# Attention's products with the values: one group for a head's 512 queries in place of two groups of 256

## The chip, the cores and the metric

The kernel runs on one core of a Trainium2 chip. The metric is the device time of one execution in microseconds; three runs of the kernel before gave 909.68, 910.4 and 912.59, median 910.4. The profile is one further execution, taken by the hardware profiler. In it PE is TensorE's matmul, PEld its weight load, DVE VectorE, ACT ScalarE, POOL GpSimd and SP SyncE, which only issues DMAs here.

## The reference

One encoder block on 512 tokens of width 2048. A modulated RMS norm is projected into two mixers that run side by side: dilated window attention with 16 heads of 64, and a gated linear attention with 4 heads. Both are gated, concatenated, projected, added to the input through a gate and normalised. The change is in the attention:

```python
for window, dilation in DILATED_PATTERNS:          # (128,1), (512,4), (2048,16)
    o_p, lse_p = dilated_window_attention(aq, ak, av, rel_bias, window, dilation)
mix_w = jax.nn.softmax(jnp.stack(lses, axis=0), axis=0)
att = jnp.einsum('pbsh,pbshe->bshe', mix_w.astype(av.dtype), jnp.stack(outs, axis=0))
```

Three softmaxes that are merged by their denominators are one softmax over a row's keys, in which a key counts as often as patterns contain it. So for each head the kernel needs scores, one softmax, and the product of its weights with the values, out[query] = sum over keys of p[query, key] v[key].

## The kernel before

**Precision.** A product of two float32 matrices is made from parts: a high part that ACT writes as fp32r, and a low part that DVE gets by subtracting it. The projections take three products (high by high, high by low, low by high). For the values, vv holds in its 128 stationary columns both parts side by side (64 high, 64 low), and the probabilities are multiplied part by part. The two halves of the output's partitions are added at the end.

**Stages.** The start (condition sums, norm, the projection of the values and of four heads' queries and keys) takes until about 187 us. Then four units follow, qk2, qk4, qk6 and gk. Each is a projection of 192 products of 512 columns, and each carries the attention of four heads. Later units (values and gates of the linear attention, then the output projection) take the rest.

**Tokens and tiles.** Tokens are sorted by parity (the queries' order is the reverse of the keys'); a tile i is 128 queries. Of 512 keys a tile needs 416: three whole chunks of 128 and a rest of 32. Tile 0 has chunks 1, 2, 3 and a rest in chunk 0; tile 1 chunks 2, 3, 0 and a rest in 1; tile 2 chunks 3, 0, 1 and a rest in 2; tile 3 chunks 0, 1, 2 and a rest in 3.

**A head's work.** Each of these is an item of the list that attention() makes:
- score (lines 819 to 856): two products of 416 columns into a PSUM tile s; two DVE operations add the bias and take the minimum (L837), ACT takes the exponential (L841), DVE the reciprocal (L844), POOL the scaling (L854). With a score goes one piece of side work for DVE, a token sum (S) or a sum for the value bias (vbias).
- turn (858 to 876): three transposes on PE into t (L871); ACT writes the high part (L875), DVE the low part (L876). The turn of tile 3 first does rest (879 to 890): one transpose r of the four 32-key rests (L882), two copies on ACT (L888), two subtractions on DVE (L890), and the same again.
- values (892 to 907): for each pair of tiles e, eight products of 256 columns (L899), four chunks by two parts, from a tile pts[e] that holds both parts and has blocks of zeros where a tile has no keys in the chunk. The rests come last. Then ACT copies half of the output (L902) and DVE adds it to the other half into cat (L906).

**What sets the order.** PE's instructions stand as the program is written. A unit counts a tick for every three of its 192 products, and an item is put in when its place, spread evenly from 0.185 on over 0.8 of the unit, is reached; the last one falls into the next unit. On the other engines a scheduler of the framework orders the instructions when the program is built, and each runs its queue in order. SP issues its DMAs in order too. PSUM has three buffers for s, t and o together. Weights are fetched by SP, split by ACT (L491) and DVE (L475), some groups of 24 products ahead.

Of the kernel before, what the change touches and what calls it, by code (L numbers as in the profile page):

```python
# [18 lines left out]
P = 128  # L19
S = 512  # L20
D = 2048
KT = D // P
# [57 lines left out]
def _runs():  # L80
# [109 lines left out]
def block_kernel(ctx: ExitStack, tc: tile.TileContext, a: dict):  # L190
    nc = tc.nc
# [7 lines left out]
    sm = mid.enter_context(tc.tile_pool(name="sm", bufs=4))  # L199
# [303 lines left out]
    spl, psb, vraw, vv, sqs = {}, {}, {}, {}, {}  # L503
# [131 lines left out]
    for i, (st, k) in enumerate(sets[1:], 1):  # L635
        e = "ab".index(st)
# [15 lines left out]
    for z in range(2):  # L652
        c = slice(512 * z, 512 * z + 512)
# [31 lines left out]
    n = len(chain) // 2  # L685
# [54 lines left out]
    ident = const("ident", [P, P])  # L740
# [49 lines left out]
    cat = [None] * 4  # L790
# [13 lines left out]
            return go[1]()  # L804

    pts = []

    def attention(pairs):

        tiles = [(2 * p + j, i) for p in pairs for j in range(2) for i in range(4)]  # L810
        gt, pr_ = {}, {}
        heads = [2 * p + j for p in pairs for j in range(2)]

        def g_load(h):
            g = gp.tile([P, 896], F32, tag="g", name=f"g{h}")
            nc.sync.dma_start(g[:, :768], bass.AP(grow.tensor, grow.offset + h * 1024, [[2, P], [1, 768]]))
            gt[h] = g

        def score(h, i):
            def go():  # L820
# [12 lines left out]
                st = sm.tile([P, 4], F32, tag="st", name=f"st{h}{i}", bufs=6)  # L833
                least = 3e38
                for z, (lo, hi, at) in enumerate(BIAS_AT[i]):
                    to = st[:, 0:1] if hi == NK else st[:, 3:4]
                    top = nc.vector.tensor_tensor_reduce(  # L837
                        out=t[:, lo:hi], in0=ps[:, lo:hi], in1=gt[h][:, at:at + 2 * (hi - lo) - 1:2], op0=ALU.add, op1=ALU.min,
                        scale=1.0, scalar=least, accum_out=to).ins
                    least = to  # L840
                act(t, t, AF.Exp, bias=st[:, 0:1], scale=-1.0, accum_out=st[:, 1:2])  # L841
                held = beside(top)
                with tc.issue_after(held) if held else nullcontext():
                    nc.vector.reciprocal(st[:, 2:3], st[:, 1:2])  # L844
                todo_ = [(t, t)]
                if i % 2:
                    todo_ = [(t[:, :384], t[:, :384]), (pr_[h, 0][:, 96 - 32 * i:128 - 32 * i], t[:, 384:416])]
                elif i:
                    todo_ = [(t[:, 32:], t[:, 32:]), (pr_[h, 0][:, 32:64], t[:, :32])]
                for to, of in todo_:  # L850
                    if (h, i) in ((15, 2), (15, 3)):
                        act(to, of, AF.Copy, scale=st[:, 2:3])
                    else:
                        last["pool"] = nc.gpsimd.tensor_scalar(to, of, st[:, 2:3], 1.0, op0=ALU.mult, op1=ALU.mult).ins  # L854
                pr_[h, i] = tile_
            return go

        def turn(h, i):
            def go():
                e, half = divmod(i, 2)  # L860
                if len(pts) == e:
                    pts.append(B8(f"pt{e}", [2, 4, 256], F32R))
                    nc.gpsimd.memset(pts[e][:, :, 3, 0:P].bitcast(F32), 0.0)
                    nc.gpsimd.memset(pts[e][:, :, 0, P:2 * P].bitcast(F32), 0.0)
                if i == 3:
                    rest(h)
                pt, t = pts[e], pr_.pop((h, i)) if i else pr_[h, i]
                pk = PA(f"t{h}{i}")
                first_ = 0 if half else 128
                for kt in range(3):  # L870
                    nc.tensor.transpose(pk[:, kt * P:kt * P + P], t[:, first_ + kt * P:first_ + kt * P + P], ident)  # L871
# [3 lines left out]
                act(hi, src, AF.Copy)  # L875
                tt(lo, src, hi.bitcast(F32), op=ALU.subtract)  # L876
            return go

        def rest(h):

            pk = PJ(f"r{h}")
            nc.tensor.transpose(pk[:, :P], pr_.pop((h, 0))[:, 0:128], ident)  # L882
            for e in range(2):
                at = 64 - 64 * e
                of = pk[at:at + 32, :P], pk[at + 32:at + 64, :P]
                to = [(pts[e][0:32, w, 0, P:2 * P], pts[e][96:128, w, 3, 0:P]) for w in range(2)]
                for z in range(2):
                    act(to[0][z], of[z], AF.Copy)  # L888
                for z in range(2):
                    tt(to[1][z], of[z], to[0][z].bitcast(F32), op=ALU.subtract)  # L890

        def values(h, e):
            def go():
                t = pts[e]
                po = PA(f"o{h}{e}")
                order = (1, 2, 3, 0)
                for n_, c in enumerate(order):
                    for w in range(2):
                        mm(po[:, :256], vv[h // 4][:, CHUNK_OF[e][c], h % 4, :], t[:, w, c, :],  # L899
                           start=n_ == 0 and w == 0, stop=n_ == 3 and w == 1)  # L900
                oh = sm.tile([64, 256], F32, tag="oh", name=f"oh{h}{e}", bufs=1)
                act(oh, po[64:128, :256], AF.Copy)  # L902
                own = stacks[h][3]
                p = h // 2
                dst = cat[p // 4][own, p % 4, :].rearrange("p (c e) -> p e c", e=2)[:, 1 - e, :]
                tt(dst[:, ::-1], po[0:64, :256], oh, op=ALU.add)  # L906
# [48 lines left out]
    def shift_row():  # L955

        pt_ = PA("pshift")
        nc.tensor.transpose(pt_[:KT, :P], shift, ident)
        t = sm.tile([KT, P], F32, tag="oh", name="shiftt", bufs=1)
# [708 lines left out]
    for pair, (l, r) in enumerate(OUT_PAIRS):  # L1668
# [17 lines left out]
        v = keep(f"v{pair}", g1)  # L1686
# [100 lines left out]
```

## Time and profile before

| | |
|---|---|
| runs | 909.68, 910.4, 912.59 us; median 910.4 |
| the profiled execution, first to last instruction | 907.1 us (its own time around this is not told) |
| granted PE clock | 0.997 |
| PE busy | 893.3 us, 98% |
| DVE busy | 730.9 us, 81% |
| ACT busy | 498.2 us, 55% |
| the four units with attention | 187 to 445 us |

Busy PE time is not PE at its peak: products overlap, and a row's duration is longer than the distance to the next. How long an instruction occupies PE is read from start to start. In rows of the timeline the columns are start, duration, engine, line, operation, output and inputs, shapes, count, and in brackets the idle time ahead of it with what ended it.

### The profile page before, as it was taken

The page shows a single profiled execution, that of the slowest core. Times are in us where ns is not written, and L with a number is a line of the kernel's source. Part 1 is how long each engine was busy: PE and PEld are TensorE (multiplying, and loading weights), DVE is VectorE, ACT ScalarE, POOL GpSimd, SP SyncE. Part 2 cuts the span into 40 slices and gives each one's busy share as a digit, 9 for nine tenths or more (in the row PEclk, how much of TensorE's full clock was granted, in tenths as well). Part 3 has the DMA queues.
Part 4 walks back from the last instruction along what each step waited for, and adds up shares of the span by engine and source line. Part 5 has one row for each costly group of instructions (what it writes and reads, how often), then busy time and mean ns, then how long its engine had stood idle before and what let it go on. Part 6 is the DMA issues. An engine that isn't in the chain of part 4 may idle for free.

```text
span 907.1 us, 12545 instructions
## 1 busy us (share of the span) xinstructions
PE 893.3 (98%) x4279; PEld 744.4 (82%) x4279; DVE 730.9 (81%) x1236; ACT 498.2 (55%) x859; POOL 120.8 (13%) x218
## 2 busy tenths in 40 slices
PE   8999999999999999999999999999999999999996
PEld 6888888888888888888878888888888888888884
DVE  7998899878889888888668668595787559797787
ACT  5553533566656755656657554373664248455464
POOL 0000000023323233133100101112020100000001
PEclk9999999999999999999999999999999999999998
DMA  9999498587797897998878869678797987877863
GB/s 350 403 413 405 177 370 308 172 249 215 218 267 244 233 261 226 251 271 229 281 232 258 316 201 314 204 241 267 234 277 206 277 282 284 291 284 255 298 231 145
DMA packets 64203, 241.30 MB, mean 266 GB/s; under 512 B 8358, under 2 KB 10694, under 8 KB 54538
## 3 DMA queue, kind: packets, MB, share of 16 engines
q1 hardware_dynamic: 57378, 198.18, 61.2%
q0 software_dynamic: 6464, 42.01, 19.6%
q8 instruction: 34, 0.56, 0.2%
q10 hardware_dynamic: 296, 0.30, 0.1%
q14 instruction: 31, 0.25, 0.1%
HBM read 224.64 MB, written 51.47 MB: 304 GB/s over the span
## 4 chain that ended last, share of the span: by engine, by line
PE 55%; DVE 2%; ACT 1%; issue 1%; DVEq 0%; ACTq 0%
PE g L230 4%; PE g L228 4%; PE g L229 4%; PE ps_ag L230 3%; PE ps_ag L228 3%; PE ps_ag L229 3%; PE ps_gv_P L228 3%; PE ps_gv_P L229 3%; PE ps_gv_P L230 3%; PE ps_gg L228 2%; PE ps_gg L229 2%; PE ps_gg L230 2%; PE go L1102 2%; PE ps_gk L228 2%; PE ps_gk L229 2%; PE ps_gk L230 2%
## 5 line engine op out<-in xcount | busy, mean ns | idle before, releaser
L854 POOL TENSOR_SCALAR p<-p,st 128x32 f32<-128x32 f32 (+2 forms) x108 | 55.0, 519 | 167.4 <-DVE st L844 120.7
L326 DVE CUSTOM_DVE_ANT_0 cb<-cb,sb,c_bcond 128x2048 f32<-128x2048 f32 (+1 forms) x32 | 73.4, 2295 | 1.9 <-DMA cb<-in_wm 1.7
L841 ACT ACTIVATE p<-p,st 128x416 f32<-128x416 f32 x64 | 41.1, 642 | 46.7 <-DVE st L837 38.9
L427 POOL DMA_DIRECT2D T<-in_w_o x32 | 23.1, 724 | 159.2 <-ACT V2h L491 10.8
L876 DVE TENSOR_TENSOR pt<-t,pt 128x384 fp32r<-128x384 f32 x64 | 35.3, 551 | 3.9 <-ACT pt L875 3.0
L875 ACT ACTIVATE pt<-t 128x384 fp32r<-128x384 f32 x64 | 31.3, 488 | 12.7 <-PE t L871 11.7
L899 PEld LDWEIGHTS o<-pt,vv 128*128 128x128 f32 x256 | 34.9, 190 | 3.7 <-DVE pt L890 0.6
L899 PE MATMUL o<-pt,vv 128*128 128x256 f32 x256 | 36.3, 283 | 0.3 <-DVE pt L890 0.2
L871 PE MATMUL t<-c_ident,p 128*128 128x128 f32 x192 | 31.3, 272 | 0.0
L871 PEld LDWEIGHTS t<-c_ident,p 128*128 128x128 f32 x192 | 24.3, 140 | 7.9
L837 DVE CUSTOM_DVE_ANT_0 p<-s,g,st 128x256 f32<-128x256 f32 x64 | 27.6, 432 | 1.7
L837 DVE CUSTOM_DVE_ANT_0 p<-s,g 128x160 f32<-128x160 f32 x64 | 23.4, 366 | 4.9 <-PE s L830 3.9
L829 PE MATMUL s<-ks,qh 128*128 128x416 f32 x64 | 22.9, 358 | 0.3 <-DVE pt L876 0.3
L326 DVE CUSTOM_DVE_ANT_0 rawg<-rawg,crow,gate 128x1024 f32<-128x1024 f32 x16 | 20.4, 1280 | 2.9 <-DMA rawg<-in_wg 2.9
L830 PE MATMUL s<-ks,ql 128*128 128x416 f32 x64 | 22.4, 351 | 0.0
L1070 ACT ACTIVATE sq<-st,sc 128x256 f32<-128x256 f32 x24 | 12.2, 506 | 18.4 <-DVE st L1060 9.9
L427 POOL DMA_DIRECT2D T3V<-in_w_gv x8 | 5.5, 684 | 126.0 <-ACT qk21h L491 119.8
L1560 POOL TENSOR_SCALAR x<-x,rn 128x512 f32<-128x512 f32 x2 | 2.3, 1168 | 148.2 <-ACT rn L1549 143.7
L888 ACT ACTIVATE pt<-r 32x128 fp32r<-32x128 f32 x64 | 17.1, 268 | 8.2 <-DVE pt L890 3.4
L326 DVE CUSTOM_DVE_ANT_0 rawg<-rawg,crow,c_bcond 128x1024 f32<-128x1024 f32 x16 | 20.3, 1278 | 0.7 <-DMA rawg<-in_wg 0.7
L890 DVE TENSOR_TENSOR pt<-r,pt 32x128 fp32r<-32x128 f32 x64 | 18.2, 285 | 1.8 <-ACT pt L888 0.7
L427 POOL DMA_DIRECT2D T<-T x16 | 8.9, 559 | 79.3 <-ACT V8h L491 12.9
(1660 smaller groups left out, 3115.3 us busy)
## 6 DMA issues: line engine op xcount, KB each, us to landing
cb<-in_wm SPq DMA_DIRECT2D x31, 1024.0 KB, 8.7
T<-in_w_o POOLq DMA_DIRECT2D x32, 512.0 KB, 6.3
rawg<-in_wg SPq DMA_DIRECT2D x32, 512.0 KB, 6.0
raw_O<-in_w_o SPq DMA_DIRECT2D x32, 512.0 KB, 4.7
raw_qk<-in_w_qk SPq DMA_DIRECT2D x24, 512.0 KB, 4.3
raw_O<-T SPq DMA_DIRECT2D x24, 512.0 KB, 5.5
rawb<-in_w_sb SPq DMA_DIRECT2D x16, 512.0 KB, 5.5
rawv<-in_wv SPq DMA_DIRECT2D x16, 512.0 KB, 4.8
```

What stands on the lines that cost most here:

```text
L228: mm(ps, lh, rh, start=first, stop=False, skip_group_check=more)
L229: mm(ps, ll, rh, start=False, stop=False, skip_group_check=more)
L230: mm(ps, lh, rl, start=False, stop=last, skip_group_check=more)
L326: return nc.vector.tensor_tensor_reduce(out=w, in0=w, in1=with_, op0=ALU.mult, op1=ALU.add, scale=1.0, scalar=init, accum_out=dst)
L427: move = nc.gpsimd.dma_start(dst, src, max_dma_last_dim=8192, **how).ins
L837: top = nc.vector.tensor_tensor_reduce(out=t[:, lo:hi], in0=ps[:, lo:hi], in1=gt[h][:, at:at + 2 * (hi - lo) - 1:2], op0=ALU.add, op1=ALU.min,
L841: act(t, t, AF.Exp, bias=st[:, 0:1], scale=-1.0, accum_out=st[:, 1:2])
L854: last["pool"] = nc.gpsimd.tensor_scalar(to, of, st[:, 2:3], 1.0, op0=ALU.mult, op1=ALU.mult).ins
L871: nc.tensor.transpose(pk[:, kt * P:kt * P + P], t[:, first_ + kt * P:first_ + kt * P + P], ident)
L875: act(hi, src, AF.Copy)
L876: tt(lo, src, hi.bitcast(F32), op=ALU.subtract)
L899: mm(po[:, :256], vv[h // 4][:, CHUNK_OF[e][c], h % 4, :], t[:, w, c, :], start=n_ == 0 and w == 0, stop=n_ == 3 and w == 1)
```

## The change

A head's probabilities now lie in two tiles, one for the high part and one for the low part, with 16 slots of 128 queries each, so that the tiles' blocks for one key chunk stand at equal distances. One group of nine products makes all 512 queries of a head: chunks 1 and 2 for all four tiles (512 columns, both parts), chunk 0 for tiles 1 to 3 and chunk 3 for tiles 0 to 2 (384 columns, both parts). The rests of tiles 1 and 2 stand in slots 11 and 2 among whole blocks, with 96 rows of zeros. The rests of tiles 0 and 3 get slots 14 and 15: there both parts stand below each other in one tile's rows, and a ninth product of 256 columns multiplies them with rest_v, which holds those 32 rows of the values twice. Four DMAs of 32 rows a unit fill rest_v from vv. Output copy and addition are done once a head, for 512 columns; the copy's buffer now comes from the pool of general 512-column tiles. An item list of 36 replaces that of 40.

```diff
-CHUNK_OF = ((1, 2, 3, 0), (3, 0, 1, 2))
+FULL = (((2, 0), (3, 5), (1, 10)), ((2, 1), (0, 4), (3, 7)), ((0, 6), (3, 9), (1, 12)), ((2, 3), (0, 8), (1, 13)))
+RUN_OF = ((1, 0, 4, 10, 1), (2, 0, 4, 0, 1), (0, 1, 4, 4, 2), (3, 0, 3, 5, 2))
+REST_OF = (14, 11, 2, 15)
...
+    def rest_load(w):
+        t = rest_v[w] = kp.tile([P, 4, P], F32R, tag="rv", name=f"rv{w}")
+        for z in range(4):
+            of = vv[w][96:128, 0] if z < 2 else vv[w][0:32, 3]
+            nc.sync.dma_start(t[32 * z:32 * z + 32].bitcast(F32), of.bitcast(F32))
...
-                e, half = divmod(i, 2)
-                if len(pts) == e:
-                    pts.append(B8(f"pt{e}", [2, 4, 256], F32R))
...
+                if not pts:
+                    for z in "hl":
+                        pts.append(B8(f"pt{z}", [16, P], F32R))
...
-                hi = pt[:, 0, half:half + 3, P * half:P * half + P]
-                lo = pt[:, 1, half:half + 3, P * half:P * half + P]
+                at, step = FULL[i][0][1], FULL[i][1][1] - FULL[i][0][1]
+                hi, lo = (pt[:, at:at + 2 * step + 1:step, :] for pt in pts)
...
+            hi, lo = pts
+            to = [(hi, 0, hi, 32), (hi, 0, lo, 0), (hi, 96, lo, 96), (hi, 64, hi, 96)]
+            parts = [(t[a:a + 32, REST_OF[i], :], u[b:b + 32, REST_OF[i], :], pk[96 - 32 * i:128 - 32 * i, :P])
+                     for i, (t, a, u, b) in enumerate(to)]
+            for pair in (parts[:2], parts[2:]):
+                for up, _, of in pair:
+                    act(up, of, AF.Copy)
+                for up, low_, of in pair:
+                    tt(low_, of, up.bitcast(F32), op=ALU.subtract)
...
-        def values(h, e):
+        def values(h):
             def go():
-                t = pts[e]
-                po = PA(f"o{h}{e}")
-                order = (1, 2, 3, 0)
-                for n_, c in enumerate(order):
-                    for w in range(2):
-                        mm(po[:, :256], vv[h // 4][:, CHUNK_OF[e][c], h % 4, :], t[:, w, c, :],
-                           start=n_ == 0 and w == 0, stop=n_ == 3 and w == 1)
-                oh = sm.tile([64, 256], F32, tag="oh", name=f"oh{h}{e}", bufs=1)
-                act(oh, po[64:128, :256], AF.Copy)
+                po = PA(f"o{h}")
+                for n_, (c, a0, a1, at, step) in enumerate(RUN_OF):
+                    for pt in pts:
+                        mm(po[:, P * a0:P * a1], vv[h // 4][:, c, h % 4, :], pt[:, at:at + (a1 - a0 - 1) * step + 1:step, :],
+                           start=n_ == 0 and pt is pts[0], stop=False, skip_group_check=True)
+                mm(po.rearrange("p (i q) -> p i q", i=4)[:, 0:4:3, :], rest_v[h // 4][:, h % 4, :], pts[0][:, 14:16, :],
+                   start=False, stop=True, skip_group_check=True)
+                oh = T2(f"oh{h}", parts=64)
+                act(oh, po[64:128], AF.Copy)
...
-        for x in range(n + 4):
+        for x in range(n + 3):
...
-            if v >= 0 and v % 4 < 2:
-                items.append(values(tiles[v][0], v % 4))
+            if v >= 0 and v % 4 == 0:
+                items.append(values(tiles[v][0]))
...
+        rest_load(heads[0] // 4)
```

DVE's queue around the first head (head 0, in qk2). Names: pt, pth and ptl are the tiles of the probabilities' parts, t and r the transposes, p and st a score's tile and its minimum and sum, S1e a token sum, qk25l the low part of a weight; the lines of the changed kernel are some ten further down. Before:

```order
L837 ISA p_1748,st_1749<-s_1745,g_1624 128x256
L837 ISA p_1748,st_1749<-s_1745,g_1624,st_1749 128x160
L1207 TENSOR_TENSOR S1e_1753<-h_lo 128x512
L475 TENSOR_TENSOR qk25l<-raw_qk_1668,qk25h 128x1024
L890 TENSOR_TENSOR pt_1673<-r_1761,pt_1673 32x128
L844 RECIPROCAL st_1749<-st_1749 128x1
L890 TENSOR_TENSOR pt_1673<-r_1761,pt_1673 32x128
L837 ISA p_1792,st_1793<-s_1789,g_1624 128x160
L876 TENSOR_TENSOR pt_1729<-t_1771,pt_1729 128x3x128
L890 TENSOR_TENSOR pt_1729<-r_1761,pt_1729 32x128 x2
L837 ISA p_1792,st_1793<-s_1789,g_1624,st_1793 128x256
L906 TENSOR_TENSOR cat_1607<-o_1805,oh_1814 64x256
```

and of the change:

```order
L477 TENSOR_TENSOR qk25l<-raw_qk_1673,qk25h 128x1024
L847 ISA p_1757,st_1758<-s_1754,g_1629,st_1758 128x160
L1220 TENSOR_TENSOR S1e_1762<-h_lo 128x512
L902 TENSOR_TENSOR pth<-r_1779,pth 32x128
L854 RECIPROCAL st_1758<-st_1758 128x1
L902 TENSOR_TENSOR ptl<-r_1779,pth 32x128
L847 ISA p_1801,st_1802<-s_1798,g_1629 128x160
L887 TENSOR_TENSOR ptl<-t_1789,pth 128x3x128
L847 ISA p_1801,st_1802<-s_1798,g_1629,st_1802 128x256
L902 TENSOR_TENSOR ptl<-r_1779,pth 32x128
L1226 TENSOR_TENSOR S_1734<-S_1734,S1e_1762 128x512
L902 TENSOR_TENSOR pth<-r_1779,pth 32x128
```

The same instructions stand ahead of the first rest's subtraction, with the weight's split moved up into the score; the third and fourth subtraction of the rests went behind half a score and a token sum.

PE's queue at the second head, from the transpose of its rests on. Before:

```order
L882 MATMUL r_1924<-c_ident,p_1717 128x128
L871 MATMUL t_1934<-c_ident,p_1836 128x128 x3
L228 MATMUL ps_qk_2_1561<-h_hi,qk24h 128x512
L229 MATMUL ps_qk_2_1561<-h_hi,qk24l 128x512
L230 MATMUL ps_qk_2_1561<-h_lo,qk24h 128x512
L228 MATMUL ps_qk_3_1562<-h_hi,qk24h 128x512
L229 MATMUL ps_qk_3_1562<-h_hi,qk24l 128x512
L230 MATMUL ps_qk_3_1562<-h_lo,qk24h 128x512
L829 MATMUL s_1946<-ks_1539,qh_1542 128x416
L830 MATMUL s_1946<-ks_1539,ql_1543 128x416
L228 MATMUL ps_qk_3_1562<-h_hi,qk24h 128x512
```

and of the change:

```order
L882 MATMUL t_1935<-c_ident,p_1849 128x128 x3
L230 MATMUL ps_qk_3_1567<-h_hi,qk24h 128x512
L231 MATMUL ps_qk_3_1567<-h_hi,qk24l 128x512
L232 MATMUL ps_qk_3_1567<-h_lo,qk24h 128x512
L839 MATMUL s_1944<-ks_1539,qh_1542 128x416
L840 MATMUL s_1944<-ks_1539,ql_1543 128x416
L230 MATMUL ps_qk_0_1564<-h_hi,qk25h 128x512
L231 MATMUL ps_qk_0_1564<-h_hi,qk25l 128x512
L232 MATMUL ps_qk_0_1564<-h_lo,qk25h 128x512
L909 MATMUL o_1965<-pth,vv_980 128x512
L909 MATMUL o_1965<-ptl,vv_980 128x512
```

Before, nine products of the projection and a score stand between tile 3's transposes and the first product of the values; now there are six and a score. In a unit's first and third head there are nine, as before; in its last head there are 15.

More of the change, by code (lines that the diff above doesn't have):

```diff
@@ L806, in block_kernel @@
     pts = []
+    rest_v = {}
+    def rest_load(w):
[3 more added lines that the diff above has]
+            nc.sync.dma_start(t[32 * z:32 * z + 32].bitcast(F32), of.bitcast(F32))
     def attention(pairs):
@@ L859, in go @@
             def go():
-                e, half = divmod(i, 2)
-                if len(pts) == e:
-                    pts.append(B8(f"pt{e}", [2, 4, 256], F32R))
-                    nc.gpsimd.memset(pts[e][:, :, 3, 0:P].bitcast(F32), 0.0)
-                    nc.gpsimd.memset(pts[e][:, :, 0, P:2 * P].bitcast(F32), 0.0)
+                if not pts:
+                    for z in "hl":
+                        pts.append(B8(f"pt{z}", [16, P], F32R))
+                        for at, to in ((2, 3), (11, 12)) + ((14, 16),) * (z == "h"):
+                            nc.gpsimd.memset(pts[-1][:, at:to, :].bitcast(F32), 0.0)
                 if i == 3:
                     rest(h)
-                pt, t = pts[e], pr_.pop((h, i)) if i else pr_[h, i]
+                t = pr_.pop((h, i)) if i else pr_[h, i]
                 pk = PA(f"t{h}{i}")
-                first_ = 0 if half else 128
-                for kt in range(3):
-                    nc.tensor.transpose(pk[:, kt * P:kt * P + P], t[:, first_ + kt * P:first_ + kt * P + P], ident)
-                hi = pt[:, 0, half:half + 3, P * half:P * half + P]
-                lo = pt[:, 1, half:half + 3, P * half:P * half + P]
+                first_ = 0 if i % 2 else 128
+                for n_, (c, _) in enumerate(FULL[i]):
+                    kt = (c - i - 1) % 4
+                    nc.tensor.transpose(pk[:, n_ * P:n_ * P + P], t[:, first_ + kt * P:first_ + kt * P + P], ident)
+                at, step = FULL[i][0][1], FULL[i][1][1] - FULL[i][0][1]
+                hi, lo = (pt[:, at:at + 2 * step + 1:step, :] for pt in pts)
                 src = pk[:, :3 * P].rearrange("p (k q) -> p k q", k=3)
@@ L882, in rest @@
             nc.tensor.transpose(pk[:, :P], pr_.pop((h, 0))[:, 0:128], ident)
[L883 to L890, printed above, removed]
@@ L903, in go @@
                 own = stacks[h][3]
                 p = h // 2
-                dst = cat[p // 4][own, p % 4, :].rearrange("p (c e) -> p e c", e=2)[:, 1 - e, :]
-                tt(dst[:, ::-1], po[0:64, :256], oh, op=ALU.add)
+                dst = cat[p // 4][own, p % 4, ::-1].rearrange("p (c e) -> p e c", e=2)
+                tt(dst, po[0:64].rearrange("p (e c) -> p e c", e=2), oh.rearrange("p (e c) -> p e c", e=2), op=ALU.add)
             return go
@@ L958, in shift_row @@
         nc.tensor.transpose(pt_[:KT, :P], shift, ident)
-        t = sm.tile([KT, P], F32, tag="oh", name="shiftt", bufs=1)
+        t = T2("shiftt", parts=KT)[:, :P]
         act(t, pt_[:KT, :P], AF.Copy)
```

## The prediction

> **What bounds the kernel now.** I read the page first, then the stretches, then PE's order of time around one head, then the two engines that feed it.
>
> ```profile
> PE   893.3 (98%) x4279; PEld 744.4 (82%) x4279; DVE 730.9 (81%) x1236; ACT 498.2 (55%) x859; POOL 120.8 (13%) x218
> ```
> ```profile
> 187.00:251.00 64.00, 64.00 (x338) 54.51 (x337) 54.64 (x151) 40.74 (x91) 19.30 (x38) 1.00 0.84 234
> 251.00:316.00 65.00, 64.68 (x343) 54.55 (x342) 56.57 (x157) 39.36 (x90) 18.86 (x36) 1.00 0.84 249
> 316.00:381.00 65.00, 64.72 (x346) 55.01 (x345) 57.10 (x159) 39.83 (x90) 19.65 (x36) 1.00 0.87 246
> 381.00:445.00 64.00, 63.97 (x342) 54.57 (x342) 53.66 (x151) 41.01 (x92) 17.25 (x32) 1.00 0.88 260
> ```
>
> The second fence is the view of busy time by stretch; the columns behind the length are PE, weight loads, DVE, ACT and POOL, then the granted clock. Its rows are the four units that carry attention (heads 0 to 3, 4 to 7 and so on). There PE has no idle time worth the name, at the full clock, and DVE is busy for 54 to 57 of 64 or 65 us, about 86%. So the bound is PE's stream, second by second; a PE instruction that goes is a gain, and an instruction of PE that waits is a loss that nothing returns. DVE is close behind: a chain through its queue is never served at once.
>
> **What the products themselves save.** PE around the first head, in order of time (start, duration):
>
> ```profile
> 206.58 0.27 PE L882 MATMUL r<-c_ident,p 128*128 128x128 f32 x1
> 206.69 0.49 PE L871 MATMUL t<-c_ident,p 128*128 128x128 f32 x3
> ...
> 208.79 0.39 PE L228 MATMUL ps_qk<-h_hi,qk23h 128*128 128x512 f32 x1
> 209.02 0.39 PE L229 MATMUL ps_qk<-h_hi,qk23l 128*128 128x512 f32 x1
> 209.24 0.39 PE L230 MATMUL ps_qk<-h_lo,qk23h 128*128 128x512 f32 x1
> 209.47 1.11 PE L899 MATMUL o<-pt,vv 128*128 128x256 f32 x8
> 210.42 0.40 PE L228 MATMUL ps_qk<-h_hi,qk23h 128*128 128x512 f32 x1
> ```
>
> From start to start, eight products of 256 columns take 0.95 us, 0.119 each; 512 columns take 0.227 (208.79 to 209.47, three of them), and 384 lie between, 0.173. A head costs 16 x 0.119 = 1.90 now. After the change it costs 4 x 0.227 + 4 x 0.173 + 0.119 for the rest's 256 columns = 1.72. That is 0.18 a head, **2.9 us** for 16. The columns only fall from 4096 to 3840, so this is all there is on PE.
>
> The Trainium skill, "TensorE: Matmul & The Clock Gate", section "Back-to-back issue gap", gives columns / 2.4 GHz plus 2.5 ns for products that follow each other at the full clock: 109 ns for 256 columns where this trace has 119, and 216 for 512 where it has 227. Estimated by that rule the saving would be 2.0 us; the trace decides, and I keep its durations.
>
> **What the products now wait for.** Before, a head's two groups were apart: the first needs the rests only in its last four of eight products, the second, which needs tile 3, starts some 4.5 us later (7.3 us behind the rest's transpose in the first head). Now the one group starts where the first stood or earlier, and its second product already reads the low part of tile 3 (slot 13) and of tile 1's rest (slot 11). The fourth reads tile 2's rest, the ninth the last rest. All these come through ACT and DVE: two copies, two subtractions, two copies, two subtractions, and tile 3's own pair between. What that chain takes, for the first head (DVE, then ACT):
>
> ```profile
> 206.04 0.56 DVE L876 TENSOR_TENSOR pt<-t,pt 128x384 fp32r<-128x384 f32 x1 [0.21 <-ACT pt L875]
> 206.51 0.41 DVE L837 CUSTOM_DVE_ANT_0 p<-s,g 128x256 f32<-128x256 f32 x1
> ...
> 207.28 0.69 DVE L1207 TENSOR_TENSOR S1e<-h_lo 128x512 f32<-128x512 f32 x1
> 207.92 1.23 DVE L475 TENSOR_TENSOR qk25l<-raw_qk,qk25h 128x1024 fp32r<-128x1024 f32 x1
> 209.18 0.28 DVE L890 TENSOR_TENSOR pt<-r,pt 32x128 fp32r<-32x128 f32 x1
> ...
> 210.14 0.55 DVE L876 TENSOR_TENSOR pt<-t,pt 128x384 fp32r<-128x384 f32 x1
> 211.21 0.48 DVE L837 CUSTOM_DVE_ANT_0 p<-s,g,st 128x256 f32<-128x256 f32 x1
> ```
> ```profile
> 206.83 1.06 ACT L491 ACTIVATE qk25h<-raw_qk 128x1024 fp32r<-128x1024 f32 x1 [0.82 <-ACT pt L875]
> 207.91 0.27 ACT L888 ACTIVATE pt<-r 32x128 fp32r<-32x128 f32 x1
> ...
> 209.13 0.49 ACT L875 ACTIVATE pt<-t 128x384 fp32r<-128x384 f32 x1
> 209.95 0.55 ACT L888 ACTIVATE pt<-r 32x128 fp32r<-32x128 f32 x2 [0.33 <-DVE pt L890]
> ```
>
> Counted from the rest's transpose (206.58), tile 3's low part is done at 4.11 us. In the new order the group stands 2.89 behind that transpose in a unit's first and third head (the same nine 512-column products, transposes and score products lie between), 2.21 in the second head (three fewer), and 3.87 in the last (15 products, no scores). So the second product is due at 3.12, 2.44, 3.12 and 4.10, the fourth 0.45 later, the ninth 1.37 later.
>
> First head, from both sides. Between tile 2's subtraction (done at 206.60) and the first rest's (209.18), DVE still has one score's two parts, a token sum and a weight split, 2.6 us in the rows above. The tile 2 transposes now stand three products (0.68) further ahead of the rest's. If DVE makes use of all of it, tile 3 is done at 3.45 and PE waits 0.33; if of none, at 4.11 and it waits 1.0. Then 0.48 of a score part stands ahead of the third rest (order above), which ends 0.76 behind tile 3, while the fourth product comes 0.45 behind the second: 0.3 more. So 0.6 to 1.3; I take 1.2, because DVE's queue reaches that point through the same instructions as before.
>
> Second head: tile 3 has the least time, and a whole score (0.86) and, on ACT, a weight split (1.06) now stand ahead of the third rest.
>
> ```profile
> 220.44 0.27 PE L882 MATMUL r<-c_ident,p 128*128 128x128 f32 x1
> ```
> ```profile
> 222.63 0.56 DVE L876 TENSOR_TENSOR pt<-t,pt 128x384 fp32r<-128x384 f32 x1
> ```
>
> Tile 3 ends at 2.75 as the rows stand, 0.3 too late; the score and the rest (0.28) make it 3.9 where the fourth product is due at 3.2: 1.0 in all. With an empty DVE queue tile 3 would be done by 2.1, the score by 3.0 and the rest by 3.3, against 2.89: 0.4. I take 0.7 here, and more in qk4 and qk6 (1.2 and 1.4), where a bias sum of 1.2 us, as the one that puts off tile 3 at 367.65 below, stands inside the chain, and 0.7 in gk.
>
> ```profile
> 365.74 1.22 DVE L977 CUSTOM_DVE_ANT_0 rawv<-rawv,shb 128x1024 f32<-128x1024 f32 x1
> 367.65 0.55 DVE L876 TENSOR_TENSOR pt<-t,pt 128x384 fp32r<-128x384 f32 x1
> ```
>
> Third head: 0 with an empty queue, 1.1 to 1.9 with the queue of before; 0, 0.5, 0.6, 0.3. First heads: 1.2, 1.2, 0.2, 0.2, since in heads 8 and 12 the order has the first rests and tile 3 side by side, with no score part between. Last heads: nothing, 3.87 is enough. The sum is 2.8 + 4.0 + 1.4 = **8.2 us**. Bounds: with a queue that is empty when each chain begins 6.1; with before's delays (tile 3 done 2.75 to 4.98 behind the transpose in these twelve heads, first 210.14, mean 4.08, against a mean due time of 2.89) 12 x 1.19 = 14.2.
>
> What goes: three of the 32 groups waited already, together 0.8 us, such as this one:
>
> ```profile
> 273.54 0.75 PE L899 MATMUL o<-pt,vv 128*128 128x256 f32 x5
> 274.49 0.62 PE L899 MATMUL o<-pt,vv 128*128 128x256 f32 x3 [0.20 <-DVE pt L890]
> ```
>
> **What costs nothing.** Two evictions of 256 columns become one of 512:
>
> ```profile
> L906 DVE TENSOR_TENSOR cat<-o,oh 64x256 f32<-64x256 f32 x32 | 13.2, 413 | 1.9 <-ACT oh L902 1.5
> L902 ACT ACTIVATE oh<-o 64x256 f32<-64x256 f32 x32 | 12.2, 382 | 6.0 <-PE o L899 5.2 <-ACT pt L888 0.2
> ```
>
> By the 64x512 forms of the same engines (L777 688 ns, L776 593 ns) that is 0.14 us of DVE and 0.17 of ACT a head, under PE's stream; without that cover at most 2.2 and 2.7 in all. The first wait of this kind that it could remove is DVE's backlog, but the subtraction into cat now waits for all nine products and stands ahead of the next head's first tile, so I give it nothing. The sixteen small loads of rest_v stand in SP's queue ahead of weight loads:
>
> ```profile
> 169.15 4.25 SPq L374 DMA_DIRECT2D raw_qk<-in_w_qk  x2
> 256.01 0.34 SPq L374 DMA_DIRECT2D raw_qk<-in_w_qk  x1
> ```
> ```profile
> 169.71 1.27 DVE L623 SCALAR_TENSOR_TENSOR vv<-vraw,rcol,vv 128x256 fp32r<-128x256 f32 x3
> ```
> ```profile
> 189.39 1.06 ACT L491 ACTIVATE qk22h<-raw_qk 128x1024 fp32r<-128x1024 f32 x1
> 262.74 1.06 ACT L491 ACTIVATE qk44h<-raw_qk 128x1024 fp32r<-128x1024 f32 x1 [1.02 <-PE ps_qk L230]
> ```
>
> The first pair waits for the first part of vv (170.2), 1 us behind the weight load at 169.15 that it now precedes, and that weight is first read at 189.39. Later ones wait for the last head's products of the unit before and hold up a load such as that of 256.01, whose weight is read 6.7 us later, by four issues, about 1.3 us by the row's 0.34. Nothing; if the loads were late by all of that, 1.3 in each of three units.
>
> The Trainium skill, "Perfetto Trace Analysis", section "Optimizing Scalar/DVE Operations", says that grouping operations pays where the engine is saturated, and that breaking them up lets work finish sooner where ACT and DVE leave gaps on another engine. Here both halves apply to the same edit; its second half is the forecast's mechanism and speaks against the change.
>
> **Sum.** 907.1 span - 2.9 - 0.8 + 8.2 = 911.6. The median of the runs is 910.4, 3.3 above this span, so 914.9: about half a per cent slower.
>
> **The rivals.**
> - *Not slower: DVE is early.* The added 0.68 us ahead of the rests and PE's own waits empty DVE's queue. Each wait then has its lower bound, or the score parts are done earlier: 4 to 6 us of waits against 3.7 gone, +0.3 to +2.4, about 911.8 as a median. For it: DVE has 14% to spare. Against it: the idle time lies at unit ends, not in the heads.
> - *Faster: the order hides it.* The chain is served at once everywhere, waits under 1 us in all: 907.1 - 3.7 + 0.5, as a median 907.2. From all I see in the order it needs a chain below 2.44 us in the second heads, where only 2.75 was ever had.
> - *Much slower: before's delays stay.* 14.2 of waits: 907.1 - 3.7 + 14.2 = 917.6, as a median 920.9. It decides as soon as DVE does not catch up. For it: twelve measured delays. Against it: PE's waits themselves give DVE time.
>
> **Chances.** Forecast (912.9 to 918) 0.45, not slower 0.26, faster 0.11, much slower 0.18. A measurement of this kernel tells 0.3%, 2.7 us, from no change. So faster 0.11, same 0.27, slower 0.62. The range is 907.6 to 921.0, which leaves out most of the faster case and the tail of the last; the forecast's own is 912 to 918.
>
> **What would show it.** The products' line should show 144 products and about 27.6 us from start to start without waits. The waits of PE should name "o <- DVE" with 6 to 10 us over 8 to 12 heads, most of it before the second and the fourth product of a group, none in last heads, and most in second heads of qk4 and qk6. PE's busy time in the four units should fall by about 0.7 each. If waits name a DMA or the score products instead, the mechanism is wrong; if PE waits less than 3 us, the chain was served sooner than any row here shows.

## The result, and the profile after

| | before | after |
|---|---|---|
| runs beside each other (4 and 4), median | 910.04 (909.26 to 912.59) | 918.07 (917.91 to 918.92) |
| ratio of the times, 95% interval | | 1.0093 [1.0079, 1.0107] |
| profiled execution, first to last instruction | 907.1 | 916.2 |
| granted PE clock | 0.997 | 0.997 |

The change costs 0.9%. Forecast were 914.9 and slower; the time lies within the range, 3.2 us above the forecast and just outside the forecast's own band (912.9 to 918).

First line of engines, kernel after:

```profile
PE 895.2 (98%) x4167; PEld 738.3 (81%) x4167; DVE 730.8 (80%) x1220; ACT 494.0 (54%) x843; POOL 122.6 (13%) x219
```

There are 112 products fewer, as the change says, and yet PE's busy time has grown by 1.9 us. Where the time went shows in what PE waits for. The waits of PE, kernel after (us in all, times, longest):

```profile
PE o L909 <- DVE ptl L887: 3.0, 7, 0.7
PE r L893 <- POOL p L864: 2.7, 3, 0.9
...
PE r L893 <- ACT p L862: 0.8, 1, 0.8
PE o L911 <- DVE pth L902: 0.5, 1, 0.5
PE o L909 <- ACT pth L900: 0.5, 1, 0.5
```

Before, this view had 0.2 us at o, 0.3 at the score products (s) and nothing at r:

```profile
PE s L829 <- DVE pt L876: 0.3, 1, 0.3
PE o L899 <- DVE pt L890: 0.2, 1, 0.2
```

Now the products with the values (o) wait for the tiles that DVE and ACT fill, and so does the transpose of the rests (r), for the scaling of the last score (on POOL; in the last unit on ACT). The rows at o and r hold 7.5 us after the change. They are too small, and the busy time too large, for one reason that the rows of the first head show. PE, then its weight loads, kernel after (start, duration):

```profile
210.67 0.39 PE L232 MATMUL ps_qk<-h_lo,qk23h 128*128 128x512 f32 x1
210.90 0.39 PE L909 MATMUL o<-pth,vv 128*128 128x512 f32 x1
211.55 0.50 PE L909 MATMUL o<-ptl,vv 128*128 128x512 f32 x1 [0.27 <-DVE ptl L887]
211.88 0.40 PE L909 MATMUL o<-pth,vv 128*128 128x512 f32 x1
212.27 0.50 PE L909 MATMUL o<-ptl,vv 128*128 128x512 f32 x1
212.60 0.34 PE L909 MATMUL o<-pth,vv 128*128 128x384 f32 x1
212.78 0.34 PE L909 MATMUL o<-ptl,vv 128*128 128x384 f32 x1
```
```profile
210.67 0.19 PEld L909 LDWEIGHTS o<-pth,vv 128*128 128x128 f32 x1
211.55 0.19 PEld L909 LDWEIGHTS o<-ptl,vv 128*128 128x128 f32 x1 [0.69 <-DVE ptl L887]
211.66 0.19 PEld L909 LDWEIGHTS o<-pth,vv 128*128 128x128 f32 x1
212.26 0.19 PEld L909 LDWEIGHTS o<-ptl,vv 128*128 128x128 f32 x1 [0.42 <-DVE ptl L902]
```

The second product starts 0.65 behind the first, where 0.227 is the distance of two that wait for nothing: 0.43 lost, of which the view books 0.27, because a row's 0.39 is longer than the distance to the next. The third follows at 0.33 instead of 0.227, and so does the one behind the fourth. So I also add up the starts: each distance between two matmul starts less what the same shape takes in an undisturbed stretch (0.227 for 512 columns, 0.190 for 416, 0.173 for 384, 0.120 for 256, 0.108 for a transpose), booked to the later of the two. In us:

| kernel | undisturbed work | over at o | over at r | over at s | first to last start |
|---|---|---|---|---|---|
| before | 878.5 | 0.9 | 0.1 | 1.7 | 896.4 |
| after | 875.3 | 9.5 | 4.3 | 0.3 | 905.6 |

The 9.2 between the two are 3.2 less work, 8.6 more at o, 4.2 more at r, 1.4 less at the score products (s), and 1.0 in small pieces elsewhere.

**The waits at o** follow the prediction's list closely. What a head's group takes over 1.72 us, the next instruction included:

| heads | measured, units qk2, qk4, qk6, gk | predicted |
|---|---|---|
| first | 0.93, 1.32, 0.00, 0.01 | 1.2, 1.2, 0.2, 0.2 |
| second | 0.84, 1.36, 1.97, 1.12 | 0.7, 1.2, 1.4, 0.7 |
| third | 0.22, 0.60, 0.89, 0.60 | 0, 0.5, 0.6, 0.3 |
| last | 0.00, 0.00, 0.00, 0.00 | 0 |
| sum | 9.9 | 8.2 |

**The wait at r** was not in the sum at all. In a unit's last head the rests' transpose needs the last score scaled. The rows of that score's second product, of DVE's reciprocal, of POOL's scaling and of the transpose, before and then after, at the end of qk2:

```profile
240.26 0.35 PE L830 MATMUL s<-ks,ql 128*128 128x416 f32 x1
...
243.58 0.15 DVE L844 RECIPROCAL st<-st 128x1 f32<-128x1 f32 x1
...
243.83 0.86 POOL L854 TENSOR_SCALAR p<-p,st 128x384 f32<-128x384 f32 x2 [2.13 <-DVE st L844]
...
245.54 0.27 PE L882 MATMUL r<-c_ident,p 128*128 128x128 f32 x1
```
```profile
243.90 0.35 PE L840 MATMUL s<-ks,ql 128*128 128x416 f32 x1
...
247.30 0.40 PE L232 MATMUL ps_qk<-h_lo,qk27h 128*128 128x512 f32 x1
...
247.42 0.14 DVE L854 RECIPROCAL st<-st 128x1 f32<-128x1 f32 x1
...
247.73 0.85 POOL L864 TENSOR_SCALAR p<-p,st 128x384 f32<-128x384 f32 x2 [4.10 <-PE ps_qk L232]
...
248.63 0.33 PE L893 MATMUL r<-c_ident,p 128*128 128x128 f32 x1 [0.94 <-POOL p L864]
```

From score product to the end of the scaling it is 4.4 us before (240.26 to 244.69) and 4.7 after (243.90 to 248.58): the chain is about as long as it was. (The scaling's row after the change names a product of PE. DVE's reciprocal, which the scaling needs too, ends at 247.56, so that product can account for 0.2 at most; in the last head of qk4 the same row names DVE's reciprocal, and PE waits as long.) But PE came to the transpose 5.28 behind that product before, 0.85 late enough, and comes to it 3.63 behind now (247.30 + 0.227). The 1.65 that are gone are a group of eight products (0.95) and three products of the projection (0.69), which stood between; PE waits 1.1. The other last heads lose 1.05, 1.09 and 0.98.

The two evictions cost less in all, as predicted (DVE 10.9 for 13.2, ACT 9.5 for 12.2), under PE's stream. Groups of lines, kernel after:

```profile
L918 DVE TENSOR_TENSOR cat<-o,oh 64x512 f32<-64x512 f32 x16 | 10.9, 684 | 4.1 <-ACT oh L914 3.8
L914 ACT ACTIVATE oh<-o 64x512 f32<-64x512 f32 x16 | 9.5, 596 | 8.6 <-PE o L911 8.4
```

### The profile page after: what moved, and what is told of

Its sections match the earlier page's. It is cut to its first block, busy times and chain, and to the rows that moved or that the text cites. A ratio compares the mean times of both kernels' runs of the same rounds, so it can differ in the third digit from the quotient of the medians.

```text
span 916.2 us, 12344 instructions
## 1 busy us (share of the span) xinstructions
PE 895.2 (98%) x4167; PEld 738.3 (81%) x4167; DVE 730.8 (80%) x1220; ACT 494.0 (54%) x843; POOL 122.6 (13%) x219
## 4 chain that ended last, share of the span: by engine, by line
PE 87%; DVE 6%; ACT 4%; issue 2%; POOL 0%; DVEq 0%; ACTq 0%
PE ps_qk L230 4%; PE ps_qk L232 4%; PE ps_qk L231 4%; PE g L232 4%; PE g L230 4%; PE g L231 4%; PE stb L232 3%; PE stb L231 3%; PE stb L230 3%; PE ps_ag L230 3%; PE ps_ag L232 3%; PE ps_ag L231 3%; PE ps_gv_P L230 3%; PE ps_gv_P L231 3%; PE sta L230 3%; PE ps_gv_P L232 3%
## 5 line engine op out<-in xcount | busy, mean ns | idle before, releaser
L886 ACT ACTIVATE pth<-t 128x384 fp32r<-128x384 f32 x64 | 31.2, 487 | 23.9 <-PE t L882 23.3
L887 DVE TENSOR_TENSOR ptl<-t,pth 128x384 fp32r<-128x384 f32 x64 | 35.3, 551 | 7.5 <-ACT pth L886 6.6
L909 PE MATMUL o<-ptl,vv 128*128 128x512 f32 (+1 forms) x64 | 24.9, 388 | 3.3 <-DVE ptl L887 3.0
L900 ACT ACTIVATE pth<-r 32x128 fp32r<-32x128 f32 x64 | 17.2, 269 | 13.4 <-PE r L893 8.3
L909 PE MATMUL o<-pth,vv 128*128 128x512 f32 (+1 forms) x64 | 23.6, 370 | 0.5 <-ACT pth L900 0.5
L1083 ACT ACTIVATE sq<-st,sc 128x256 f32<-128x256 f32 x24 | 12.2, 507 | 18.5 <-DVE st L1073 9.9
L909 PEld LDWEIGHTS o<-ptl,vv 128*128 128x128 f32 x64 | 12.0, 187 | 10.3 <-DVE ptl L887 6.2
```

What stands on the lines that cost most here:

```text
L909: mm(po[:, P * a0:P * a1], vv[h // 4][:, c, h % 4, :], pt[:, at:at + (a1 - a0 - 1) * step + 1:step, :], start=n_ == 0 and pt is pts[0], st ...
```

## The experiments

Two questions: do the products' waits come from the chain of copies and subtractions, as the prediction holds (A in the expectations), or from something else that the change brought, such as the two tiles of probabilities, the other shapes or the loads of rest_v (the rivals there)? And is it the merged products or their place that costs? Each kernel was timed against the kernel before in three rounds.

**1. The nine products read slots that are written early.** The kernel after, in which every product of a head reads slots 4 to 13 of the high tile, written by ACT's first copies; it leaves out the low parts, slots 0 to 3 and the rests' slots 14 and 15, so the attention's sums are incomplete. All copies and subtractions are still done.

```diff
-RUN_OF = ((1, 0, 4, 10, 1), (2, 0, 4, 0, 1), ...
+RUN_OF = ((1, 0, 4, 10, 1), (2, 0, 4, 10, 1), ...
-    ... pt[:, at:at + (a1 - a0 - 1) * step + 1:step, :],
+    ... pts[0][:, at:at + (a1 - a0 - 1) * step + 1:step, :],
-    ... pts[0][:, 14:16, :],
+    ... pts[0][:, 10:12, :],
```

> The changed kernel, but all nine products read blocks of the high tile that ACT has written by its first two copies (slots 4 to 13): the low tile, slots 0 to 3 and slots 14 and 15 are left out of the products, so the attention's output is not complete. Products, columns, loads and evictions stay. Theory A (the chain of copies and subtractions ahead of the products costs 9.9 us): PE waits at the products fall under 1 us, 918.1 - 9.4 = about 908.7. Rival B (nine wide products with strided operands are slower themselves) and rival C (loads of rest_v, output copies): 918 as before, since all of that stays.

Measured: 910.46 us beside 909.56, ratio 1.0005 [0.9995, 1.0014], span 909.2. By starts 0.2 are left at o, and 5.4 stand at r. The waits of PE have no row at o, and at r:

```profile
PE r L893 <- POOL p L864: 3.4, 3, 1.6
...
PE r L893 <- ACT p L862: 1.3, 1, 1.3
```

Nearly all of o's 9.5 us hang on when the late slots are written: the shapes, the two tiles and the loads of rest_v are still there, and 0.2 is left. The wait at r stays without the late slots: it is a second cause. A's number held r's 4.2 already, since it starts from the changed kernel's time; the time stays 1.8 us above it, of which 1.1 is r, which grew from 4.3 to 5.4; the rest are small pieces that were not followed.

**2. Only the place.** The kernel before with its eight and eight products of 256 columns, both groups one after the other where the first group of the changed kernel stands; the list of 36 items; nothing else.

```diff
-        for x in range(n + 4):
+        for x in range(n + 3):
...
-            if v >= 0 and v % 4 < 2:
-                items.append(values(tiles[v][0], v % 4))
+            if v >= 0 and v % 4 == 0:
+                items.append(lambda h=tiles[v][0]: [values(h, e)() for e in range(2)])
```

> The kernel before, with one edit: a head's two groups of eight products stand together at the place of the first one, with the item list of 36. No zero block goes, no product changes. Theory A: placement alone brings waits; the second group's low part of tile 3 is due 1.07 us behind the start of the first instead of 0.23, so waits at the products are about half of the changed kernel's, 4 to 6 us, and the 4.2 us at the rests' transposes of the last heads come too: 910 + 8 to 10 = 918 to 920. Rivals B and C: 910.

Measured: 917.82 us, ratio 1.0090 [1.0075, 1.0105], span 914.7; 5.7 over at o, 4.3 at r. Waits of PE:

```profile
PE o L899 <- DVE pt L890: 3.6, 6, 1.3
PE r L882 <- POOL p L854: 2.8, 3, 1.1
...
PE r L882 <- ACT p L852: 0.8, 1, 0.8
```

So the place alone, with the old products, costs what the whole change costs, the wait at r included. What the merging adds is where in the group PE meets the chain. Of the old products' 5.7, 4.6 stand ahead of the fourteenth of sixteen, which reads what the chain's last subtraction writes (L890, the low part of tile 2's rest). The merged products read the low part of tile 3 in their second product already, which costs some 4 us more at o (9.5 against 5.7), and have 3.2 less work: nearly even.

**3. Another order of the nine.** The kernel after, with the products that read early slots first: chunks 1, 0 and 3 by the high part, then 3, 0, 1 by the low part, then chunk 2, then the rests.

```diff
+PRODUCTS = ((0, 0), (2, 0), (3, 0), (3, 1), (2, 1), (0, 1), (1, 0), (1, 1))
...
-                for n_, (c, a0, a1, at, step) in enumerate(RUN_OF):
-                    for pt in pts:
+                for n_, (run, part) in enumerate(PRODUCTS):
+                    (c, a0, a1, at, step), pt = RUN_OF[run], pts[part]
```

> The changed kernel with another order of the nine products: high parts of chunks 1, 0, 3, low parts of 3, 0, 1, then chunk 2, then the rests. The low part of tile 3 is due 0.75 us behind the start instead of 0.23, tile 2's rest at 1.4 instead of 0.7. Theory A: with the delays that the changed kernel's trace shows, waits at the products fall from 9.9 to about 5 us: about 913. Rival B or C: 918.

Measured: 916.86 us, ratio 1.0081 [1.0066, 1.0096], span 914.8; 7.8 over at o, 4.7 at r. A miss: I had expected half of o's loss to go, and 1.7 of 9.5 went. The waits of PE show where it went instead:

```profile
PE o L912 <- DVE pth L903: 3.0, 4, 1.2
...
PE o L912 <- ACT p L852: 0.6, 1, 0.6
PE o L912 <- DMA S<-S: 0.6, 1, 0.6
```

L912 is the ninth product; 5.6 of the 7.8 stand ahead of it. What was late before the second is met again at the rests, which end the chain: a group of 1.7 us is short against it. (The last two rows name a releaser that has nothing to do with the rests; which instruction it was there is left open.)

**4. The transpose of the rests later.** The kernel after, with the last head's turn of tile 3 two ticks later, six products of the projection, and nothing else.

```diff
+        at[-2] += 0.031
```

> The changed kernel; in each unit the last head's turn of tile 3, with its rests' transpose, stands two ticks (six products, 1.36 us) later, and the products stay. Theory A2 (the transpose comes too early behind the scaling by POOL, 4.2 us in four units): these waits vanish, and 0.4 us a unit come at the last heads' products: 918.1 - 4.2 + 1.8 = 915.7. Rival (the wait follows from DVE's order, where the reciprocal stands behind the next heads' queries, and moves with it): 918.

Measured: 916.58 us, ratio 1.0079 [1.0064, 1.0094], span 914.2. The view of waits has no row at r any more. By starts 0.1 us is left there (4.3 before the edit), but o has 11.6 (9.5), because the last heads' values now stand nine products of the projection behind their rests, not 15, and three of the four groups take 0.7 too long. Net 2.1 by starts and 2.0 by the span: r's loss is what it seemed, and its own place decides on it; moved alone it brings half of itself back as waits at o.

**5. The values later.** The kernel after, with the values' group of a unit's first three heads 1.85 places of the list later, and the next head's first turn 0.95 later. Behind the rests' transpose there are now 15, 15, 18 and 15 products of the projection before the group, where there were 9, 6, 9 and 15. (The expectation below had counted 12 in the first and second head; the trace has 15.)

```diff
-        items = []
+        items, late = [], {}
...
+                late[len(items)] = 1.85
+                late[len(items) + 1] = 0.95
...
+        for q, places in late.items():
+            if q < len(items) - 1:
+                at[q] += places * span / len(items)
```

> The changed kernel, with the nine products of a unit's first three heads put behind six more projection products (nine in the second head, three in the third: 12 products and a score behind tile 3's transposes in the first and second head, 18 in the third), and the next head's first turn right behind them. Theory A: with the delays of the changed kernel's trace (tile 3's low part done 2.2 to 3.9 us behind the rests' transpose, the last rest 3.8 to 5.6) waits at the products fall from 9.5 to 1 us or less, with up to 1 us of new waits where a transpose needs the PSUM tile of the products back: 918 - 8 = 910. The 4.2 us at the last heads' rests stay. Rival: the scheduler orders DVE's queue anew around the new place, the chain moves back with it and the waits stay: 916 or more.

Measured: 909.62 us beside 909.34, ratio 0.9990 [0.9979, 1.0001], span 907.9; 0.1 over at o, 3.1 at r. No row of o is left among the waits; of those inside the units the largest are

```profile
PE r L893 <- POOL p L864: 2.2, 3, 0.8
...
PE ps_qk L230 <- DVE ks L779: 0.7, 2, 0.4
```

With the whole computation done, the place alone gives back o's loss.

**6. Both, by half.** The values 0.95 of a place later (12, 12, 15, 15 products), the last head's turn of tile 3 and its values two ticks later. The loop that adds the places is that of experiment 5. (The expectation below counts three products more in the third head; the trace has six.)

```diff
...
+                late[len(items)] = 0.95
+                late[len(items) + 1] = 0
...
+        at[-2] += 0.027
...
-        at[-1] += move_last
+        at[-1] += move_last + 0.032
```

> As the kernel with the later products, but only three products later in the first and third head and six in the second, the next head's first turn left in place; and in the last heads the turn of tile 3 five to six products and the products about seven later. Theory A: the waits at the rests' transposes go as in the run with the later last turn (4.2 us), waits at the products fall to about 3 us, mostly for the last rest of heads 5, 9 and 13: 918 - 4.2 - 6.5 = 907.5, just below the kernel before.

Measured: 907.08 us, ratio 0.9979 [0.9968, 0.9991], span 906.4; r is at 0.1, and o at 2.1, in heads 4 (0.95 at one product) and 9 (0.52):

```profile
PE o L909 <- DVE ptl L887: 0.8, 1, 0.8
...
PE o L911 <- DVE pth L902: 0.4, 1, 0.4
```

**7. Both, in full.** Experiment 5's distances with experiment 6's last head.

> Both moves: the products later as in the first kernel of this list, with the next head's first turn behind them, and the last heads' turn of tile 3 and products later as in the second. Theory A: waits at products and rests below 1.5 us in all, so what is left of the change is its 2.9 us and the 0.9 of waits that the kernel before has: 910 - 3 = 907, if no transpose waits for PSUM instead.

Measured: **904.58 us** (903.28 to 905.57) beside 909.34, ratio 0.9943 [0.9928, 0.9958], span 902.8. By starts 0.5 at o, 0.1 at r, 0.4 at s; 892.1 from first to last start. All that PE waits for by this view:

```profile
PE sta L590 <- ACT h_hi L534: 2.0, 1, 2.0
PE warm L296 <- DVE hot L308: 1.5, 1, 1.5
PE go L1121 <- ACT V27h L493: 0.3, 1, 0.3
```

None of them is in the attention. It is faster than the kernel before by 4.8 us and than the kernel after by 13.5 (medians of two series), whose computation it makes in another order. Expected were 907, 2.4 us more. 0.7 of that is the kernel before, which stood at 910 in the expectation and at 909.34 beside these runs; 1.3 is the loss at the score products, which goes (1.7 to 0.4) and was in no sum. That piece comes with the place: experiment 2, with the old products, has 0.4 there. Its line of engines:

```profile
PE 889.9 (99%) x4167; PEld 739.7 (82%) x4167; DVE 730.1 (81%) x1220; ACT 492.1 (55%) x843; POOL 123.1 (14%) x219
```

**8. Both, and the order of experiment 3.** The edits of experiments 3 and 7 together.

> The kernel with both moves, and the nine products in the other order (chunk 2's behind the others, low parts late). Theory A: where waits are gone already the order of the products tells nothing, within 0.1% of the kernel with both moves; where a head still waits for its low parts, up to 1 us less.

Measured: 905.67 us, ratio 0.9948 [0.9930, 0.9967], span 904.7; 0.6 at o. The intervals of 7 and 8 overlap widely: once the inputs are there, the order of the nine makes no difference that these runs can tell.

The eight kernels by starts, in us, as in the table above:

| kernel | undisturbed work | over at o | over at r | first to last start |
|---|---|---|---|---|
| 1 early slots | 875.3 | 0.2 | 5.4 | 898.5 |
| 2 only the place | 878.5 | 5.7 | 4.3 | 904.0 |
| 3 order | 875.3 | 7.8 | 4.7 | 904.1 |
| 4 turn later | 875.3 | 11.6 | 0.1 | 903.5 |
| 5 values later | 875.3 | 0.1 | 3.1 | 897.2 |
| 6 both, by half | 875.3 | 2.1 | 0.1 | 895.8 |
| 7 both | 875.3 | 0.5 | 0.1 | 892.1 |
| 8 both and order | 875.3 | 0.6 | 0.1 | 894.0 |

## Why the prediction was right, and where its sum was not

**The bound.** Right: PE's stream sets the time, and an instruction that waits on it is lost. In the ten kernels of the two tables the distance from first to last start, less work and waits at o, r and s (0.3 to 0.4 in the eight), is 15.1 to 18.3 us, while work and waits themselves go from 876 to 889.

**What the products save.** Right: 2.9 forecast. A group that waits for nothing takes 1.723 us from start to start (heads 3, 7, 8, 11, 15), 1.72 was forecast; 16 of them make 27.6. By the undisturbed distances it is 3.2, since the table takes 0.120 for 256 columns and the forecast took 0.119. The formula of the Trainium skill that stood beside this ("TensorE: Matmul & The Clock Gate", section "Back-to-back issue gap") is given there for an isolated product and not for a stream of loads and products; the trace's distances decide.

**What the products wait for.** Right in mechanism, place and nearly in size: the chain through ACT and DVE is met before the second product (4.3 us of the 9.9) and the fourth (1.6), most in the second heads of qk4 and qk6, never in a last head. Two places were smaller than these: the third product, which reads the high part of tile 2's rest and waited 0.7 for ACT's copy in the second head of qk6, and the ninth, 1.0, of which 0.7 in that head too. Experiment 1 shows the cause by taking away the late slots, experiment 5 by giving them time. 9.9 stand against 8.2: the first heads were too high by 0.5, the second and third too low by 1.3 and 0.9. Some 1.5 us of the whole are not waits themselves but the next products' late starts (14 of 0.11 each), which the step did not have.

Against this the old waits were priced at 0.8 at o, right (0.9), while a loss of 1.7 at the score products, of which 1.4 went, was not in the sum at all.

**The step that failed** is "Last heads: nothing, 3.87 is enough". It asked only whether the values find their inputs, and for them the answer was right. It did not ask what the same move does to the items around: where the list goes from 40 to 36 and a group leaves the place ahead of the last rests' transpose, that transpose comes 1.65 us sooner after its score, and its chain had only 0.85 to spare. This cost 4.2 us. Experiment 2 shows that it comes with the place, experiment 4 that six products are enough to pay for it. What the prediction asked of the products, whether their inputs are there when they come sooner, has to be asked of every item that moves up, and the transposes stood in the same view of PE's order.

So the span was forecast 4.5 above the one before and came out 9.1 above. By starts the 4.7 of difference are 4.2 at r, 1.2 at o, 1.0 in small pieces, less 1.4 at s and 0.3 of work. The median missed by 3.2 only, and that is luck. The sum added 3.3 to get from the span to the median, but in every run for which both are on record the time lies 1.7 to 1.9 above its own span. So the profiled execution of before took some 908.9 us, less than any of the four timed beside the change, and the addition was some 1.4 too large. It hid that much of the 4.6 by which the span was forecast too short.

**What costs nothing.** Right as far as the runs show it: with the merged evictions and the loads of rest_v still there, experiment 7 has no wait in the attention. DVE's saved 2.3 us have no wait in the attention there that they could shorten, so they were rightly given nothing.

**The rivals.** "Before's delays stay" gave 14.2 us of waits and 920.9; the groups lost 9.9, between that and the 6.1 of an empty queue. The time of 918.07 lies between the forecast and this rival, but r, which is not its mechanism, took it there. "DVE is early" would have had 4 to 6 us of waits, and fell with the 9.9. "The order hides it" did not happen, yet experiment 7 has what that rival supposed: with the distances, waits are nearly gone and the kernel is 4.8 us faster than before. 3.2 of this is the products' work; 1.3 at the score products came with the place. What the kernel before would gain with its items moved in the same way was not run, so no number here says what the merging alone is worth against it.

**Two tests that were badly chosen.** PE's busy time was to fall by 0.7 in each unit; over the whole it grew by 1.9. The other test fell short as well: the view of waits has 3.5 us for o <- DVE (and 0.5 for o <- ACT) where 6 to 10 were to show. Both come from how rows are drawn: a product that waited is drawn with 0.50 where another has 0.39, and short waits vanish under rows that overlap. In experiment 7, where the attention's waits are gone, PE's busy time falls by 3.4. The distances of starts are the measure.

The Trainium skill, "Perfetto Trace Analysis", section "Optimizing Scalar/DVE Operations", had been set beside the forecast for its second half, that breaking up ACT's and DVE's instructions may let work finish sooner where these two cause gaps on other engines. What is grouped here are PE's products, and the gaps did not come from their size: experiment 2, whose products are not merged, is as slow as the change, and experiment 7, whose products are, is the fastest. Not the grouping itself cost most of the time but the due date that it moved.

## What to carry to other kernels

Where a change gathers two groups on a full engine into one, the gathered group is due when its earliest part was, but the last of its inputs comes no sooner than before: price the distance to the last input, and move the group by that much. Then go through every other item that the move lets come sooner, and compare its distance from its own producer with the chain behind it; here the one that was not looked at cost half as much as the one that was. Read waits of a pipelined engine from start to start, not from idle time or busy time.

## What the runs showed of the hardware that was not expected

A product that waits costs more than its wait. In the fence of the first head the product behind a waiting one starts 0.33 us later, not 0.227: 0.108 more, and in the kernel after this stands 14 times (334 to 343 ns from start to start), some 1.5 us. The weight loads in the second fence suggest why. In the running stream a load starts 0.23 ahead of its product (210.67 and 210.90); of a product that waits, the load starts with the product (211.55), and the next load 0.11 behind it (211.66), so a part of a load's 0.19 lies open. No run tested this alone.

Why does the load wait? It reads vv, which was complete 27 us before. The last write of vv, on DVE, kernel after:

```profile
183.74 0.48 DVE L625 SCALAR_TENSOR_TENSOR vv<-vraw,rcol,vv 128x256 fp32r<-128x256 f32 x1
```

Only the moving operand ptl was late. But the trace's records keep with each instruction the semaphores that it waits for, and in the kernel after none of the 4167 products has such a wait, while 603 of their weight loads do; the load at 211.55 itself waits for DVE's semaphore. So the program's wait for a product's moving operand stands on the weight load ahead of it, and the load is held back with its product by that.

The Trainium skill, "TensorE: Matmul & The Clock Gate", section "Step-by-step: what each phase is for", says that PE pulls weight loads ahead of products in flight. The trace agrees where nothing waits, with the 0.23 above. The load at 211.55 is no case against it, because it had a wait of its own; whether a load would run ahead if the wait stood on the product, no run here shows.
